# The weight split is emitted at the head of each step, ahead of the step's other work

## The chip, the cores and the metric

The kernel runs on one core of one Trainium2 chip. The metric is the time of one execution in microseconds (us): 2224.38 us, the median of three runs of the kernel before (2222.93 to 2225.11). A core has several engines, each with its own queue of instructions, which it works off in order: TensorE (PE in the profile) multiplies matrices, VectorE (DVE) and ScalarE (ACT) do elementwise work, GpSimd (POOL) does some elementwise work and issues some transfers, SyncE (SP) issues transfers. They wait for one another by semaphores.

## The reference

One decoder block on x of 256 tokens by 2048 channels, in float32, cut here to its chain:

```python
p = x @ w_in                          # 2048 x 9776, columns for all heads and gates
a = diff_attention(p)                 # 8 heads, value width 128 each
n = nsa_attention(p)                  # 16 heads, 4 KV groups: compressed, selected, window
m = sigmoid(g_da) * (a @ w_branch_da) + sigmoid(g_nsa) * (n @ w_branch_nsa)
h = layer_norm(alpha * x + m @ w_out)
# PEER: product keys choose 16 of 128 x 128 experts for each of 8 heads
s1, s2 = q1 @ sub_k1.T, q2 @ sub_k2.T         # q = h @ w_q
eid, gate = top16(top16(s1) + top16(s2))      # expert numbers, softmax of the scores
y = sum over heads, k: gate * gelu(u[eid] . h) * v[eid]
out = layer_norm(alpha * h + y)
```

u and v have 16384 rows (experts) of 2048 channels each. The tokens together choose so many rows that the kernel streams all of u and v and computes every expert for every token: act = gelu(u h), times a matrix G of 16384 experts by 256 tokens that holds the gates (zero where an expert was not chosen), and then G-weighted act times v.

## The kernel before

**One stream of weights.** All large matrices (w_in, the branch matrices, w_out, w_q, u, v) pass through one object W of class Stream as tiles of 128 partitions by 1024 float32 (512 KB). SyncE loads them into three raw buffers. TensorE multiplies in a rounded form of float32, so each tile is *split* into two: hi, a rounding cast by ACT (L98), and lo, the rest raw minus hi by DVE (L99). A tile has two halves of 512 columns, each with a cast and a subtraction; lo waits for hi. In a part of the program (`W.share`) GpSimd does the subtraction of the second half. The pools of hi and lo hold six halves, three tiles. A product is three passes, hi by hi, lo by hi, hi by lo; a tile takes 24 matmuls of 256 columns (in the v pass 12 of 512).

**One step a tile.** `step(fn)` handles one tile. `W.take()` hands out the tile whose turn it is (its split was emitted in an earlier step), `fn` emits its matmuls, and `W.ahead()` emits the split of the tile two places on (and the loads for which a raw buffer is free).

**Everything else rides on the steps.** Attention, top-k, the building of G and the weight split of the v pass are cut into slots (cost, pre, post), queued with `bg`. A step earns a credit (1 as a rule) and takes a slot when it has credit; the slot's pre (elementwise work) is emitted before the matmuls of the tile, its post (TensorE work) after them. Two more lists exist: `deferred` holds evacuations of PSUM, emitted by `flush()` at the start of the next step; `late` holds evacuations that are emitted in the next step after the slots (as `now`). There is no scheduler: instructions stand in each engine's queue in the order in which the code emits them.

**Stages in time**, from the profile: to 150 us the first columns of x @ w_in; to 350 the differential attention beside more of them; some 385 to 515 the NSA attention beside the gate columns; to 735 the merge, w_out and the first norm; to 970 w_q, and the first of u beside the top-k work; 970 to 1190 u beside the building of G; to 1500 the rest of u; to 2200 v; then the second norm.

**The attention pipeline.** `pipeline` (slots) has for unit k in one slot: pre does the softmax (`u_softmax`, L510 to L527) of unit k-1, the evacuation of the transposed weights (`u_evac`, L548 to L554) of unit k-3, the output (`u_out`, L584) of unit k-5; post does the logits of unit k, transposes (tp, L539) of k-2, pv of k-4.

**The G stage.** `g_onehot(q)` (pre; L1202, L1204) makes on DVE, from keys and gates in slotT, one-hot matrices `one` and `ob` for four tokens; `g_mm(q-1)` (post) multiplies those of the slot before into a bank `lg`, with eight small matmuls; its `ev` goes to `deferred` and is emitted first in the next step:

```python
V.scalar_tensor_tensor(g0[:, 0:n0, ts], gv[:, 0:n0, :], 1.0 / GSCALE, g0[:, 0:n0, ts], op0=OP.mult, op1=OP.mult)   # L1219
if n0 < HI:
    A.activation(g0[:, n0:HI, ts], gv[:, n0:HI, :], AF.Copy, scale=1.0 / GSCALE)   # L1222
A.activation(g1[:, :, ts], gv[:, HI:I2, :], AF.Copy, scale=1.0 / GSCALE)           # L1223
```

There are 64 such q; a slot costs GCOST = 1.05. In this stage a finished accumulator of u (every fourth step) is also evacuated in the flush, by a gelu on ACT (L1255) and a store that ACT issues (L1259).

Of the kernel before, what the change touches and what calls it, by code (L numbers as in the profile page):

```python
# [130 lines left out]
def block_kernel(ctx, tc, x, xT, w_in, rel_bias, onehot, lamq, lamk, subln_g, pe, w1, w2k, w2v, cmask,  # L131
# [11 lines left out]
    W = Stream(nc, stream, 3, 6)  # L143
# [6 lines left out]
    def flush(every=False):  # L150
        for q in (deferred, late) if every else (deferred,):
            for f in q:
                f()
            q.clear()

    def step(fn, credit=1.0):
        part = W.take()
        flush()
        now, late[:] = list(late), []
        state["c"] = min(state["c"] + credit, 2.0)  # L160
        post = None
        while credit and slots and state["c"] > 0 and post is None:
            cost, pre, post = slots.pop(0)
            state["c"] -= cost
            if pre:
                pre()
        for f in now:
            f()
        W.ahead()
        fn(*(part or ()))  # L170
        if post:
            post()
# [607 lines left out]
    for name, form, width, j, half in plan:  # L780
        if name == "x":
            step(lambda: None, half)
            continue
        if name == "w1":
            step(lambda hi, lo, kv=width, jj=j: w1_step(kv, jj, hi, lo), 0)
            continue
# [21 lines left out]
        if form == "T":  # L808
            def fn(hi, lo, j=j, half=half):
                if j == 0 and half == 0:  # L810
                    acc["b"] = [bank("acc", 4) for _ in range(2)]
                mm_T(acc["b"], hi, lo, xhi, xlo, 2 * j + half, 15)
            step(fn, 0.5 if name == "qd0" and j == 0 else 1)
            if j == 7:
                def ev(name=name, b=acc["b"]):
                    evac_T(name, b, 0)
                    late.append(lambda: evac_T(name, b, 1))
                late.append(ev)
        else:
            def fn(hi, lo, j=j, width=width):  # L820
                if j == 0:
                    acc["b"] = [bank("acc", 4) for _ in range(2)]
                mm_N([b[:, :width] for b in acc["b"]], hi, lo, xhi, xlo, 2 * j, (0, 1))
            step(fn, width / 512)
            if j == 7:
                late.append(lambda name=name, width=width, b=acc["b"]: evac_N(name, width, b))
# [677 lines left out]
```

## Time and profile before

| | |
|---|---|
| median of 3 runs | 2224.38 us (2222.93 to 2225.11) |
| profiled execution | 2224.97 us |
| its span | 2223.2 us |
| mean granted TensorE clock | 0.996 |
| busy: TensorE, weight loads | 2184.4 us (98%), 2016.0 us (91%) |
| busy: DVE, ACT, GpSimd | 1452.2 us (65%), 1130.3 us (51%), 246.5 us (11%) |
| chain that ended last | PE 75%, DVE 8%, DMA 5%, ACT 2% |
| 16 DMA engines | 424.72 MB, mean 191 GB/s |

The span runs from the first to the last instruction of the profiled execution; its own time is a little longer. Busy times are sums over instructions on an engine; matmuls overlap in the pipeline, so a busy TensorE is one with matmuls in flight. The granted clock is 1.00 where TensorE runs at 2.4 GHz, its higher level; the lower is 1.2 GHz. The chain is followed back from the last instruction, at each step to what released it.

### The profile page before, as it was taken

How to read it: one execution, taken by the hardware profiler on the slowest of the kernel's cores; microseconds unless marked ns; L12 is line 12 of the kernel's file. 1: busy time of each engine (PE TensorE's matmuls, PEld its weight loads, DVE VectorE, ACT ScalarE, POOL GpSimd, SP SyncE). 2: the span in 40 equal slices, each digit the busy share in tenths (PEclk: the TensorE clock that was granted, in tenths of full speed). 3: DMA queues.
4: the chain of work that ended last, by engine and by line, in shares of the span. 5: the costliest groups of instructions: out<-in, count | busy, mean ns of one | idle time of the engine just before them, and what ended most of it. 6: DMA issues, size and time to landing. Idle time of an engine off the chain costs nothing.

```text
span 2223.2 us, 40705 instructions
## 1 busy us (share of the span) xinstructions
PE 2184.4 (98%) x15712; PEld 2016.0 (91%) x15712; DVE 1452.2 (65%) x2898; ACT 1130.3 (51%) x2153; POOL 246.5 (11%) x223
## 2 busy tenths in 40 slices
PE   9999999999999999999999999999999999999997
PEld 9988999999987999999999999998888888888786
DVE  5558774665767889988886555555555555555567
ACT  5555654665545444455554444445555455554443
POOL 2002234443001501210000000000000000000002
PEclk9999999999999999999999999999999999999999
DMA  7664564545675766555656666666666666667774
GB/s 243 195 186 155 173 198 130 166 151 162 202 226 160 238 183 189 181 185 181 182 183 190 196 194 194 193 197 206 196 191 194 193 193 196 192 197 236 253 220 143
DMA packets 119843, 424.72 MB, mean 191 GB/s; under 512 B 13876, under 2 KB 14212, under 8 KB 119392
## 3 DMA queue, kind: packets, MB, share of 16 engines
q1 hardware_dynamic: 111600, 398.90, 58.0%
q0 software_dynamic: 5600, 18.75, 2.8%
q10 hardware_dynamic: 2448, 4.46, 0.5%
q8 instruction: 123, 2.02, 0.4%
q14 instruction: 72, 0.59, 0.1%
HBM read 413.37 MB, written 8.69 MB: 190 GB/s over the span
## 4 chain that ended last, share of the span: by engine, by line
PE 75%; DVE 8%; DMA 5%; ACT 2%; issue 2%; POOL 1%; ACTq 0%; DVEq 0%; POOLq 0%; SPq 0%
PE acc L191 43%; PE o L191 27%; DVE lo L99 4%; PE lg L191 2%; DMA raw<-in_v_dram 2%; DMA raw<-in_w_in_dram 1%; PE pv L191 1%; DMA raw<-in_wout_dram 1%; DMA raw<-in_wq_dram 1%; ACT hi L98 1%; PE tp L539 1%; DVE eq L1107 0%; DVE eid L1111 0%; DVE st L901 0%; DVE r L933 0%
## 5 line engine op out<-in xcount | busy, mean ns | idle before, releaser
L99 DVE TENSOR_TENSOR lo<-raw,hi 128x512 fp32r<-128x512 f32 (+1 forms) x1422 | 980.8, 719 | 551.2 <-ACT hi L98 549.2
L98 ACT CAST hi<-raw 128x512 fp32r<-128x512 f32 (+1 forms) x1494 | 872.4, 617 | 692.5 <-PE o L191 267.6
L191 PE MATMUL acc<-yhi,lo 128*128 128x256 f32 x2112 | 586.7, 278 | 5.5 <-DVE lo L99 5.5
L191 PE MATMUL acc<-yhi,hi 128*128 128x256 f32 x2112 | 591.4, 280 | 0.0
L191 PE MATMUL acc<-ylo,hi 128*128 128x256 f32 x2112 | 584.1, 277 | 0.0
L191 PEld LDWEIGHTS acc<-yhi,lo 128*128 128x128 f32 x2112 | 397.0, 188 | 9.4 <-DVE lo L99 9.1
L191 PEld LDWEIGHTS acc<-yhi,hi 128*128 128x128 f32 x2112 | 396.8, 188 | 0.4 <-ACT hi L98 0.2
L191 PEld LDWEIGHTS acc<-ylo,hi 128*128 128x128 f32 x2112 | 396.7, 188 | 0.0
L191 PE MATMUL o<-lo,whi 128*128 128x512 f32 x1000 | 389.7, 390 | 0.8 <-DVE lo L99 0.8
L191 PE MATMUL o<-hi,whi 128*128 128x512 f32 x1000 | 389.4, 389 | 0.6 <-ACT hi L98 0.5
L191 PE MATMUL o<-hi,wlo 128*128 128x512 f32 x1000 | 389.1, 389 | 0.0
L191 PE MATMUL acc<-xhi,hi 128*128 128x256 f32 x1024 | 290.7, 284 | 4.2 <-ACT hi L98 4.2
L191 PE MATMUL acc<-xhi,lo 128*128 128x256 f32 x1024 | 286.5, 280 | 5.5 <-DVE lo L99 5.3
L191 PE MATMUL acc<-xlo,hi 128*128 128x256 f32 x1024 | 285.2, 279 | 0.0
L191 PEld LDWEIGHTS o<-lo,whi 128*128 128x128 f32 x1000 | 187.7, 188 | 42.0 <-DVE lo L99 3.1
L191 PEld LDWEIGHTS o<-hi,whi 128*128 128x128 f32 x1000 | 187.7, 188 | 40.9 <-ACT hi L98 1.5
L191 PEld LDWEIGHTS o<-hi,wlo 128*128 128x128 f32 x1000 | 187.7, 188 | 38.5
L191 PEld LDWEIGHTS acc<-xhi,lo 128*128 128x128 f32 x1024 | 194.1, 190 | 7.8 <-DVE lo L99 7.7
L191 PEld LDWEIGHTS acc<-xhi,hi 128*128 128x128 f32 x1024 | 194.4, 190 | 6.0 <-ACT hi L98 5.6
L191 PEld LDWEIGHTS acc<-xlo,hi 128*128 128x128 f32 x1024 | 193.9, 189 | 0.0
L1282 POOL DMA_DIRECT2D back<-act_d x17 | 9.3, 546 | 1170.5 <-DVE G L1290 607.4
L99 POOL TENSOR_TENSOR lo<-raw,hi 128x512 fp32r<-128x512 f32 x72 | 104.1, 1450 | 231.7 <-ACT hi L98 228.0
(308 smaller groups left out, 2170.3 us busy)
## 6 DMA issues: line engine op xcount, KB each, us to landing
raw<-in_u_dram SPq DMA_DIRECT2D x256, 512.0 KB, 4.1
raw<-in_v_dram SPq DMA_DIRECT2D x256, 512.0 KB, 3.6
raw<-in_w_in_dram SPq DMA_DIRECT2D x143, 512.0 KB, 4.1
raw<-in_wout_dram SPq DMA_DIRECT2D x32, 512.0 KB, 4.2
raw<-in_wbda_dram SPq DMA_DIRECT2D x16, 512.0 KB, 3.9
raw<-in_wbnsa_dram SPq DMA_DIRECT2D x16, 512.0 KB, 3.8
raw<-in_wq_dram SPq DMA_DIRECT2D x16, 512.0 KB, 4.2
raw<-in_w_in_dram SPq DMA_DIRECT2D x16, 280.0 KB, 3.0
```

Source lines behind the costliest of these rows:

```text
L98: self.nc.scalar.copy(hi[:, :w], r)
L99: (self.nc.gpsimd if self.share and b else sub).tensor_tensor(lo[:, :w], r, hi[:, :w].bitcast(F32), op=OP.subtract)
L191: PE.matmul(o, a, b, start=start, stop=stop, skip_group_check=True)
L539: PE.transpose(tp[:, 128 * b:128 * b + 128], P[:, 128 * b:128 * b + 128], ident)
L1282: GP.dma_start(t, act_d[vorder[n]])
```

## The change

In `step`, `W.ahead()` moves from behind the slots' pre and the late evacuations to ahead of them; the flush stays first:

```diff
         part = W.take()
         flush()
         now, late[:] = list(late), []
+        W.ahead()
         state["c"] = min(state["c"] + credit, 2.0)
         post = None
         while credit and slots and state["c"] > 0 and post is None:
...
                 pre()
         for f in now:
             f()
-        W.ahead()
         fn(*(part or ()))
```

Each engine has as many instructions as before. The orders on TensorE and SyncE are the same; those of DVE, ACT and GpSimd differ. In the rows below a name's number is that of its buffer; numbers differ between the versions by a few, since buffers are numbered as they are emitted. `lo_...<-raw_...` is the subtraction of half a tile.

DVE's queue in the G stage, before: the evacuation L1219, the one-hot of the slot, then the split.

```order
L1219 SCALAR_TENSOR_TENSOR G0_9652<-lg_13661,G0_9652 128x34x4
L1202 TENSOR_TENSOR one_13673<-keys_12741,slotT_9401 128x1024
L1204 TENSOR_TENSOR ob_13674<-one_13673,slotT_9401 128x512 x2
L99 TENSOR_TENSOR lo_13679<-raw_13529,hi_13678 128x512
L99 TENSOR_TENSOR lo_13683<-raw_13529,hi_13682 128x512
L1219 SCALAR_TENSOR_TENSOR G0_9652<-lg_13712,G0_9652 128x34x4
L1202 TENSOR_TENSOR one_13724<-keys_12741,slotT_9401 128x1024
L1204 TENSOR_TENSOR ob_13725<-one_13724,slotT_9401 128x512 x2
```

The same place after, from the same evacuation on (lg_13661).

```order
L1219 SCALAR_TENSOR_TENSOR G0_9662<-lg_13661,G0_9662 128x34x4
L99 TENSOR_TENSOR lo_13674<-raw_13524,hi_13673 128x512
L99 TENSOR_TENSOR lo_13678<-raw_13524,hi_13677 128x512
L1202 TENSOR_TENSOR one_13683<-keys_12751,slotT_9401 128x1024
L1204 TENSOR_TENSOR ob_13684<-one_13683,slotT_9401 128x512 x2
L1219 SCALAR_TENSOR_TENSOR G0_9662<-lg_13712,G0_9662 128x34x4
L99 TENSOR_TENSOR lo_13725<-raw_13575,hi_13724 128x512
L99 TENSOR_TENSOR lo_13729<-raw_13575,hi_13728 128x512
```

The split of the same tile (raw_13529, now raw_13524) stands between the evacuation and the one-hot, no longer behind the one-hot. ACT's queue in this stage reads L1222, L1223, the two casts hi, in both versions, with L1255 and the store between L1223 and the casts in every fourth step.

DVE's queue in the NSA attention, before: a unit's softmax (its last rows), an evacuation, an output, the split of one half, the next softmax.

```order
L527 TENSOR_TENSOR rs_5207<-rs_5207,gsig_147 128x1
L549 SCALAR_TENSOR_TENSOR wt_5211<-tp_5180,wt_5211 128x384
L584 SCALAR_TENSOR_TENSOR r1_146<-pv_5184,rs_4909,r1_146 128x64 x2
L99 TENSOR_TENSOR lo_5217<-raw_5002,hi_5216 128x512
L510 ISA P_5280,nm_5278<-lg_5252,tb_5101 128x256
```

The same place after.

```order
L527 TENSOR_TENSOR rs_5217<-rs_5217,gsig_147 128x1
L549 SCALAR_TENSOR_TENSOR wt_5221<-tp_5180,wt_5221 128x384
L584 SCALAR_TENSOR_TENSOR r1_146<-pv_5184,rs_4919,r1_146 128x64 x2
L99 TENSOR_TENSOR lo_5279<-raw_5056,hi_5278 128x512
L510 ISA P_5290,nm_5288<-lg_5252,tb_5101 128x256
```

The row of lo is that of the next tile (raw_5056 in place of raw_5002); the other rows are the same, so that each of them stands behind one more split than before.

## Rows read from the trace of the kernel before

**Rows 1.** The page, part 1: busy time, share of the span, instructions

```profile
PE 2184.4 (98%) x15712; PEld 2016.0 (91%) x15712; DVE 1452.2 (65%) x2898; ACT 1130.3 (51%) x2153; POOL 246.5 (11%) x223
```

**Rows 2.** Waits of PE: waiter, releaser, us in total, times, longest

```profile
PE acc L191 <- DVE lo L99: 11.0, 19, 1.4
PE acc L191 <- ACT hi L98: 4.2, 3, 2.4
```

**Rows 3.** Windows: stretch: us, busy time of each engine, PEclk, DMA share, GB/s

```profile
970.00:1184.00 214.00, 214.00 (x2072) 211.79 (x2072) 184.15 (x385) 113.07 (x274) 1.23 (x1) 1.00 0.58 184
1250.00:1300.00 50.00, 50.00 (x444) 50.00 (x443) 26.61 (x42) 22.77 (x41) 0.00 (x0) 1.00 0.65 192
344.59:348.08 3.49, 3.49 (x35) 3.49 (x33) 0.38 (x1) 0.00 (x0) 0.00 (x0) 1.00 0.42 150
348.08:360.69 12.61, 12.61 (x99) 12.61 (x99) 8.93 (x18) 7.30 (x13) 5.42 (x4) 0.86 0.26 84
```

**Rows 4.** Waits from 970 to 1187 us, columns as in rows 2

```profile
ACT G L1222 <- DVE G L1219: 93.4, 63, 2.7
DVE lo L99 <- ACT hi L98: 15.0, 19, 1.1
DVE G L1219 <- PE lg L191: 12.1, 29, 0.7
```

**Rows 5.** Timelines of DVE and PE near 405 us: start, duration, instruction

```profile
405.57 0.47 DVE L584 SCALAR_TENSOR_TENSOR r<-pv,rs,r 128x64 f32<-128x64 f32 x2
408.18 0.60 PE L191 MATMUL pv<-vd,wt 128*128 128x64 bf16 x15
```

**Rows 6.** Timeline of PE from 203 to 208.5 us, its waits in brackets

```profile
205.42 0.52 PE L539 MATMUL tp<-ident,P 128*128 128x128 f32 x3 [1.76 <-DVE wt L554]
207.18 0.38 PE L191 MATMUL acc<-xhi,hi 128*128 128x256 f32 x1 [0.57 <-ACT hi L98]
207.99 0.39 PE L191 MATMUL acc<-xhi,lo 128*128 128x256 f32 x1 [0.43 <-DVE lo L99]
```

**Rows 7.** Timeline of PE near 268 us

```profile
268.08 0.40 PE L191 MATMUL acc<-hi,xhi 128*128 128x280 f32 x1 [0.81 <-ACT qs L390]
```

**Rows 8.** Timeline of DVE in the G stage

```profile
971.99 0.76 DVE L1204 TENSOR_TENSOR ob<-one,slotT 128x512 f16<-128x512 f16 x2
...
1000.99 1.29 DVE L99 TENSOR_TENSOR lo<-raw,hi 128x512 fp32r<-128x512 f32 x2 [0.73 <-ACT hi L98]
1002.20 0.29 DVE L1219 SCALAR_TENSOR_TENSOR G<-lg,G 128x136 f32<-128x136 f32 x1
...
1005.37 0.68 DVE L1202 TENSOR_TENSOR one<-keys,slotT 128x1024 f16<-128x1024 f16 x1
...
1006.76 1.29 DVE L99 TENSOR_TENSOR lo<-raw,hi 128x512 fp32r<-128x512 f32 x2
1008.44 0.30 DVE L1219 SCALAR_TENSOR_TENSOR G<-lg,G 128x136 f32<-128x136 f32 x1 [0.40 <-PE lg L191]
...
1011.74 0.30 DVE L1219 SCALAR_TENSOR_TENSOR G<-lg,G 128x136 f32<-128x136 f32 x1 [0.40 <-PE lg L191]
```

**Rows 9.** Timeline of ACT in the G stage

```profile
1000.33 1.14 ACT L98 CAST hi<-raw 128x512 fp32r<-128x512 f32 x2 [0.40 <-ACT act L1255]
...
1009.21 1.14 ACT L98 CAST hi<-raw 128x512 fp32r<-128x512 f32 x2
...
1013.50 1.14 ACT L98 CAST hi<-raw 128x512 fp32r<-128x512 f32 x2 [0.40 <-ACT act L1255]
```

**Rows 10.** Timeline of PE in the G stage, the lg matmuls

```profile
974.84 0.63 PE L191 MATMUL lg<-ob,one 128*128 128x128 f16 x8
...
1004.48 0.63 PE L191 MATMUL lg<-ob,one 128*128 128x128 f16 x8
...
1007.77 0.63 PE L191 MATMUL lg<-ob,one 128*128 128x128 f16 x8
```

**Rows 11.** Line L1219: count, duration ns min/median/max, first and last start

```profile
L1219 DVE SCALAR_TENSOR_TENSOR G<-lg,G x64: 290/300/301, 976.5 to 1188.4; 128x136 f32<-128x136 f32 x64
```

## The prediction

> **What bounds the kernel now.** I read the page first: TensorE is busy for 98% of the span, VectorE (DVE) for 65%, ScalarE (ACT) for 51% [rows 1]. Whatever DVE and ACT do is therefore free as long as TensorE never stands, and a change of order on them costs only where TensorE starts to wait. The waits of TensorE on a split are small: 11.0 us in 19 waits on lo, 4.2 us in 3 on hi [rows 2]. That is all that an earlier split can give back.
>
> Next I asked stage by stage how near the other engines are to TensorE. The table of windows answers it [rows 3]: from 1250 to 1300 us (the plain steps of the u pass) DVE is busy for 26.61 of 50 us, but from 970 to 1184 us, the stage that builds G from one-hot matrices, for 184.15 of 214 us, with TensorE at 214.00. That is 86%, the tightest long stage of the program, so I looked there for who waits for whom [rows 4]: ACT's L1222 waits for DVE's L1219 63 times, 93.4 us in all, DVE's lo waits for ACT's hi only 19 times, and DVE's L1219 waits for TensorE's lg 29 times. DVE and ACT hand work to each other in every step, and DVE still finds time to wait for TensorE.
>
> **The change part by part.** Instruction counts stay the same on every engine; the change moves casts (L98) and subtractions (L99) past other work, so it has no price but waits. It matters which work. In a step the evacuations put off from the step before (flush) come first in both versions; the work pieces (pre, and the late evacuations) stood between them and the split, and now stand behind it.
>
> *Pieces with slack.* Where a stage has no flush work on DVE or ACT, the rows on these engines are the same ring as before (piece, split, piece, split), each piece now one split later. A split wants its tile two steps before TensorE uses it, so what the splits gain is not needed where TensorE does not wait for them, and what the pieces lose is paid only where TensorE waits for a piece. In the NSA attention a step's output (L584, at 405.57 us, 0.47 us long) is done 2.14 us before the next pv matmul at 408.18 [rows 5]; one more subtraction of a half tile ahead of it takes some 0.6 us (half of the pair in [rows 8]; the other half is GpSimd's here). Cost 0, bounded by 0 and, if the lead is used up in each of the stage's some 37 steps and half a subtraction stands over, 37 x 0.3 = 11 us.
>
> *Pieces without slack.* In the differential attention at 205.42 us TensorE stands for 1.76 us on wt (DVE), and then for 0.57 and 0.43 us on hi and lo of the next tile [rows 6]. There the softmax comes later by a split and the split sooner: the first wait grows to about 3.5, the second and third go. Net +0.5, between -1 and +2. At 268.08 us TensorE stands for 0.81 us on qs (ACT) [rows 7]; a cast pair more ahead of it takes at most the 1.14 us of the 512-wide pair [rows 9], the tile here is 280 wide: +0.7, between 0 and 1.1. The 15.2 us of rows 2 I count as unchanged: these waits come in bursts where DVE or ACT is overloaded, and a reordering of one burst takes no work out of it. Bounds -15 and 0; I take 0, because the ring behind them is the same one.
>
> *The G stage.* Here a step's flush holds work for DVE and ACT: L1219 (DVE), then L1222, L1223 (ACT), which empty the lg bank into G. ACT's casts of the next split stand behind L1222 in both versions. L1222 starts when L1219 ends, whatever TensorE does: L1219 at 1002.20 and again at 1008.44 us [rows 8]; the cast follows the second at 1009.21 [rows 9]. DVE's order before is L1219, one-hot (L1202, L1204 twice), lo, lo: while ACT is at L1222, L1223 and hi, DVE has the one-hot to do, and lo finds hi ready. After, it is L1219, lo, lo, one-hot: DVE stands behind L1219 until ACT has emptied its part and cast hi, with the one-hot queued behind the standing lo. L1219 of the next step is behind the one-hot on the same engine. The step on DVE and ACT becomes one ring without overlap, summed from start to start:
> L1219 to hi: 1008.44 to 1009.21, 0.77 us [rows 8, 9].
> hi to lo: 1000.33 to 1000.99, 0.66 us (a step in which DVE was waiting for hi) [rows 8, 9].
> The pair of lo: 1000.99 to 1002.20, 1.21 us [rows 8].
> The one-hot: 1005.37 to 1006.76, 1.39 us [rows 8].
> Sum 4.03 us. TensorE needs from lg to lg 1004.48 to 1007.77, 3.29 us [rows 10]. So DVE with ACT becomes the bound, and TensorE will stand for some 0.7 us in each step, before lg on ob.
> In every fourth step ACT has the gelu of a finished accumulator and the issue of its store between L1223 and hi: L1219 to hi is 1011.74 to 1013.50, 1.76 us [rows 8, 9], the ring 5.02 us.
> L1219 runs 64 times from 976.5 to 1188.4 us [rows 11], 63 intervals, 211.9 us. After: 16 with gelu x 5.02 = 80.3, 47 without x 4.03 = 189.4. The slot costs 1.05 of a credit of 1 per step, so about two plain steps fall into the stage without a slot; TensorE's 24 matmuls take 2.70 us each time (3.29 less the 0.59 of lg), I take 2 more for each, +4. Sum 273.7, that is +61.8. The stage begins with the first one-hot at 971.99 + 0.76 = 972.75, 2.1 us ahead of its lg at 974.84 [rows 8, 10]; this lead is eaten first, -2.1. Net **+59.7 us**. Bounds: 0, if the ring does not close (below), and +90, if lo starts only at the end of hi's second cast (1.14 in place of 0.66, 63 x 0.48 = 30 more); I take 0.66, which is the row in which DVE stood and waited as it will.
>
> *Behind the G stage.* From 1190 us on the pieces are the weight splits of the v pass, which are used steps later, and DVE is half idle [rows 3]: 0.
>
> **Sum.** +59.7 + 0.5 + 0.7 = +60.9. The profiled execution took 2224.97 us (span 2223.2, 1.8 around it) and gives 2285.9; it lies 0.59 above the median of the three runs, 2224.38, so I forecast 2285.
>
> **The rivals.**
> *The ring does not close; no change.* If L1222 waited for TensorE's lg and not for L1219, ACT could cast hi while DVE is elsewhere; DVE's own work of a step, 0.30 + 1.21 + 1.39 = 2.9 us, lies below the 3.29 of TensorE, and the stage keeps its time. The point from which it decides is a ring under 3.29. For it: DVE's 29 waits for lg [rows 4] show spare time. Against: at 1002.20 L1219 ran late and lg had been finished for some time, and the 63 waits of L1222 name L1219. Time 2224 to 2227.
> *The other side: faster.* If lo of the early split stands in no burst (the queue of DVE has always work and hi is done ahead), the 11.0 + 4.2 us of rows 2 go and the G stage holds: 2224.4 - 15.2 = 2209. It decides where TensorE's wait for lo is caused by the piece ahead of it and not by hi. For it: lo is the first releaser of TensorE's waits. Against: it needs the open ring of the case above as well, and the waits are single ones (19) where both engines are full.
> *The clock falls in the G stage.* TensorE's standing of 0.7 us a step could bring its granted clock to the lower level, 1.2 GHz. From 348.08 to 360.69 us the trace shows a mean granted clock of 0.86, after 3.49 us of small matmuls (35 groups) at a clock of 1.00 [rows 3]. At the lower level a step's 3.29 us of matmuls take 6.58, then TensorE is the bound again and does not stand, so that the level would come back; for half of the 63 steps the sum is 63 x (0.5 x 6.58 + 0.5 x 4.28) = 342 us in place of 211.9, +130, about 2355. Against: waits of 1.76 us as in rows 6 are longer than those expected here. The Trainium skill (TensorE: Matmul & The Clock Gate, section "A second HAM failure mode: psum-queue depth-cycling") tells of a kernel whose TensorE stands briefly between groups of matmuls and whose clock swings between the two levels for it; by that rule this case would come about. Rows of this case show the clock at 1.00 over the whole G stage only without such standing [rows 3], so they neither show nor exclude it.
> *NSA loses its lead too.* The split of this stage has its second half on GpSimd, next to DVE, and pieces come later on both; with the bound of 11 us on top the time is 2296. The Trainium skill (SBUF — State Buffer, section "Who interferes with whom") says that DVE and GpSimd share a pair of ports under an exclusive lock, so that another alignment of their instructions could lengthen either. The row of GpSimd's lo would show it by a longer duration than before; no row of before separates it.
>
> **How the numbers follow.** A run can tell a change from none at about 0.2% (4.4 us). Forecast, the ring in the G stage and little else: 0.72, 2276 to 2293. NSA in addition: 0.10, to 2300. The clock: 0.06, 2310 to 2360. No change, or a ring that closes only in the gelu steps (16 x 1.7 = 28 us): 0.08, of which 0.05 within 0.2%. Faster: 0.04. The range takes in the first two cases and the upper part of the partial ring: 2258 to 2306. Slower 0.91, same 0.05, faster 0.04.
>
> **What would show it.** In the profile after: the L1219 rows spread from about 976 to some 1250 us, 4.0 us apart and 5.0 in every fourth; DVE's lo waits for ACT's hi in nearly each of the 64 steps (1.1 us each, 2.1 in gelu steps) and no longer for lg; TensorE has waits "lg on ob" of 0.5 to 0.9 us; the stretch from 1190 on has the same length as before; the waits on lo outside the stage stay near 11 us in total; the wait on wt near 205 us grows to 3 to 4 us and the two behind it go. I am wrong if L1219's interval stays at 3.3 us, if a granted clock below 1.00 stands in the stage, or if more than 10 us come from before 970 us.

## The result: 2285.46 us, 2.8% slower

The changed kernel takes 2285.46 us (median of 5 runs, 2284.13 to 2288.82) against 2223.54 us (5 runs, 2222.31 to 2225.11) before: ratio 1.0282, 95% interval 1.0271 to 1.0294, +61.9 us. Forecast were 2285 us and a range of 2258 to 2306.

The page after, part 1, answers to [rows 1]: the same instructions, TensorE's share down by two points.

```profile
PE 2200.6 (96%) x15712; PEld 2016.0 (88%) x15712; DVE 1450.6 (64%) x2898; ACT 1136.5 (50%) x2153; POOL 239.3 (10%) x223
```

The waits of PE in the profile after (us in total, times, longest) have two releasers that were not there before, ob and nm, and two that have grown, wt (1.8 us, one wait, before) and qs (0.8 us, one wait); lo and hi [rows 2] have fallen from 15.2 to 10.3 us together.

```profile
PE lg L191 <- DVE ob L1204: 33.8, 56, 1.3
PE acc L191 <- DVE lo L99: 8.8, 15, 1.4
PE lg L191 <- DVE nm L510: 4.3, 2, 2.5
PE tp L539 <- DVE wt L554: 3.7, 2, 2.1
PE acc L191 <- ACT qs L390: 2.2, 2, 1.9
PE acc L191 <- ACT hi L98: 1.5, 3, 0.9
```

The wait on ob is the G stage. Its window after (columns as in [rows 3]): TensorE was busy for all 214.00 us of the stage before, now for 240.66 of 280 us, at a granted clock of 1.00. Behind it a plain window of 50 us of u holds 443 matmuls, where it held 444 before: a step there costs what it cost.

```profile
970.00:1250.00 280.00, 240.66 (x2158) 222.22 (x2158) 190.68 (x400) 117.09 (x284) 1.51 (x1) 1.00 0.46 146
...
1300.00:1350.00 50.00, 50.00 (x443) 50.00 (x442) 26.74 (x42) 22.70 (x41) 0.00 (x0) 1.00 0.67 197
```

The waits of that stage (970 to 1252 us) beside [rows 4]: DVE's lo now waits for ACT's hi in nearly every step, 88.0 us in place of 15.0, and the wait of L1219 for lg is gone.

```profile
ACT G L1222 <- DVE G L1219: 155.4, 64, 2.6
DVE lo L99 <- ACT hi L98: 88.0, 65, 2.1
PEld L191 <- DVE ob L1204: 44.7, 56, 1.5
PE lg L191 <- DVE ob L1204: 33.8, 56, 1.3
```

Line L1219 after, beside [rows 11]: 270.1 us from first to last, where it was 211.9.

```profile
L1219 DVE SCALAR_TENSOR_TENSOR G<-lg,G x64: 290/291/293, 979.5 to 1249.6; 128x136 f32<-128x136 f32 x64
```

One step and the gelu step behind it, on DVE's timeline after (brackets: idle time before, and what ended it), beside [rows 8]:

```profile
1004.59 0.29 DVE L1219 SCALAR_TENSOR_TENSOR G<-lg,G 128x136 f32<-128x136 f32 x1
1006.00 1.29 DVE L99 TENSOR_TENSOR lo<-raw,hi 128x512 fp32r<-128x512 f32 x2 [1.12 <-ACT hi L98]
1007.21 0.68 DVE L1202 TENSOR_TENSOR one<-keys,slotT 128x1024 f16<-128x1024 f16 x1
...
1008.61 0.29 DVE L1219 SCALAR_TENSOR_TENSOR G<-lg,G 128x136 f32<-128x136 f32 x1
1011.02 1.29 DVE L99 TENSOR_TENSOR lo<-raw,hi 128x512 fp32r<-128x512 f32 x2 [2.12 <-ACT hi L98]
...
1013.63 0.29 DVE L1219 SCALAR_TENSOR_TENSOR G<-lg,G 128x136 f32<-128x136 f32 x1
```

From L1219 to L1219 it is 4.02 and 5.02 us (4.03 and 5.02 forecast): 1.41 us to lo, 1.21 for the pair, 1.40 for the one-hot.

The waits on nm, wt and qs are in the attention. PE's timeline after near the places of [rows 6, 7], and one new place at 392 us:

```profile
202.19 1.77 PE L191 MATMUL lg<-kdT,qdT 64*128 64x256 f32 x8 [2.47 <-DVE nm L510]
206.03 0.88 PE L539 MATMUL tp<-ident,P 128*128 128x128 f32 x3 [2.07 <-DVE wt L554]
...
250.07 0.52 PE L539 MATMUL tp<-ident,P 128*128 128x128 f32 x3 [1.67 <-DVE wt L554]
...
269.25 0.40 PE L191 MATMUL acc<-hi,xhi 128*128 128x280 f32 x1 [1.88 <-ACT qs L390]
...
392.14 0.47 PE L191 MATMUL lg<-khi,qs 128*128 128x512 f32 x1 [1.85 <-DVE nm L510]
```

The logits of a unit need the lg banks that the softmax of the unit before empties (L510). With a split ahead of it the softmax comes late, and TensorE waits for the bank before it can even reach the transposes. It stood for 2.47 us, did eight small matmuls and stood for 2.07 us. Its granted clock fell behind the first of the two: the mean from 202 to 205 us was 0.70, and from 205 to 208 us it was 0.50, the lower level. In the profile before, both windows have 1.00.

```profile
202.00:205.00 3.00, 1.77 (x8) 1.31 (x8) 1.77 (x10) 2.40 (x9) 0.51 (x1) 0.70 0.56 175
205.00:208.00 3.00, 1.97 (x10) 2.00 (x11) 2.32 (x5) 1.46 (x3) 1.61 (x4) 0.50 0.03 5
```

Where the time went, by the start of the same TensorE work in both profiles: the first lg matmul of the G stage came at 974.84 before and is 2.8 us later after, the last (1187.76) 59.0 us later; the v pass begins 59.2 us later, and the span is 59.1 us longer. So in this pair of profiles 56.2 us of the 59.1 lie in the G stage.

### The profile page after: what moved, and what is told of

It is laid out like the page before. It is cut to its first block, busy times and chain, and to the rows that moved or that the text cites. A ratio compares the mean times of both kernels' runs of the same rounds, so it can differ in the third digit from the quotient of the medians.

```text
span 2282.3 us, 40732 instructions
## 1 busy us (share of the span) xinstructions
PE 2200.6 (96%) x15712; PEld 2016.0 (88%) x15712; DVE 1450.6 (64%) x2898; ACT 1136.5 (50%) x2153; POOL 239.3 (10%) x223
## 4 chain that ended last, share of the span: by engine, by line
PE 62%; DVE 16%; ACT 6%; DMA 4%; issue 3%; POOL 0%; ACTq 0%; DVEq 0%; POOLq 0%; SPq 0%
PE acc L191 33%; PE o L191 27%; DVE lo L99 8%; ACT hi L98 2%; DVE one L1202 2%; DMA raw<-in_v_dram 2%; DVE ob L1204 1%; DMA raw<-in_w_in_dram 1%; PE pv L191 1%; PE lg L191 1%; ACT G L1223 1%; DMA raw<-in_wq_dram 1%; DMA raw<-in_wout_dram 1%; DVE G L1219 1%; ACT G L1222 1%
## 5 line engine op out<-in xcount | busy, mean ns | idle before, releaser
L99 POOL TENSOR_TENSOR lo<-raw,hi 128x512 fp32r<-128x512 f32 x72 | 97.7, 1360 | 238.1 <-ACT hi L98 237.2
```

Source lines behind the costliest of these rows:

```text
L99: (self.nc.gpsimd if self.share and b else sub).tensor_tensor(lo[:, :w], r, hi[:, :w].bitcast(F32), op=OP.subtract)
```

## The experiments

The theory: in the G stage DVE and ACT close a ring (L1219, ACT's part, hi, lo, one-hot, and L1219 of the next step) in which each piece waits for the one before. It takes 4.0 us a step, and TensorE, at 3.29, has to wait. The rival: the one-hot behind the split on DVE's queue is the loss by itself, whatever ACT does. For what is left outside the stage there are two candidates, the attention and the top-k work.

**Only the G stage.** In `step`, the other steps keep the old place:

```diff
+        g = bool(slots) and slots[0][0] == GCOST
+        if g:
+            W.ahead()
...
-        W.ahead()
+        if not (g):
+            W.ahead()
```

> The new order only in the steps of the G stage, the old order in all others. Theory (in the G stage DVE and ACT form a ring of 4.01 us a step against TensorE's 3.29): the whole loss comes back, +56 to +58 us on the kernel before, 2280 to 2282 us, with L1219 every 4.0 us and 5.0 us in gelu steps. Rival (the loss is spread over the program, a few us per stage, because pieces come later everywhere): less than +45.

Measured: 2277.8 us against 2222.89 of the kernel before in the same series, ratio 1.0249 (1.0234 to 1.0265), +54.9. The line of L1219 runs for 270.3 us, as in the changed kernel:

```profile
L1223 DVE SCALAR_TENSOR_TENSOR G<-lg,G x64: 290/292/294, 972.8 to 1243.1; 128x136 f32<-128x136 f32 x64
```

The stage alone is nine tenths of the loss; the time is 2 us below the expected band.

**All but the G stage**, the same edit with `not g`.

> The new order in all steps except those of the G stage. Theory: the G stage keeps its 212 us, and what is left is the sum of small shifts that the profile after shows (2.8 us late at the first lg matmul, then 0.9 won back in the v pass): +1 to +4 us, 2225 to 2227.5 us. Rival (the split that comes sooner takes waits away outside the G stage): at or below 2223 us. Rival (loss spread over the program): over 2235 us.

Measured: 2231.08 us, ratio 1.0038 (1.0025 to 1.0050), +8.2 against 2222.89. The G stage keeps its 212.2 us (983.4 to 1195.6). What is left outside is more than expected, though less than the rival of a spread loss, and about three times the 2.8 us that the pair of profiles shows (the interval is 5.6 to 11 us). That the earlier split wins something on balance outside the stage is refuted. Where these 8 us lie is taken up again below, with att_only.

**The casts ahead of the flush.** In the steps of the G stage only, on top of the change; DVE's order is untouched (`cast_ahead`, not shown, casts both halves of the next tile, and its split then uses these casts):

```diff
         part = W.take()
+        if slots and slots[0][0] == GCOST:
+            W.cast_ahead()
         flush()
```

> The changed kernel with one thing more: in the G stage ACT's two casts hi are emitted ahead of the flush, so that they stand before L1222 and no longer behind it; DVE's order is the changed one (L1219, lo, lo, one-hot). Theory (the ring closes through ACT: L1219, L1222, hi, lo): the ring is open, lo no longer stands behind L1219, a step takes TensorE's 3.3 us, 2226 to 2231 us. Rival (the one-hot behind the split on DVE's queue is the loss, whatever ACT does): L1219 still every 4.0 us, 2280 to 2290 us.

Measured: 2230.81 us, ratio 1.0036 (1.0023 to 1.0050). The loss of the stage is gone; what is left agrees with that of all_but_g. DVE's timeline shows the changed order at TensorE's pace, 3.3 us a step, and DVE has time to wait for lg again (L1234 is L1219 there):

```profile
1003.19 0.30 DVE L1234 SCALAR_TENSOR_TENSOR G<-lg,G 128x136 f32<-128x136 f32 x1 [0.40 <-PE lg L206]
1003.41 1.28 DVE L102 TENSOR_TENSOR lo<-raw,hi 128x512 fp32r<-128x512 f32 x2
1004.61 0.68 DVE L1217 TENSOR_TENSOR one<-keys,slotT 128x1024 f16<-128x1024 f16 x1
...
1006.49 0.30 DVE L1234 SCALAR_TENSOR_TENSOR G<-lg,G 128x136 f32<-128x136 f32 x1 [0.40 <-PE lg L206]
```

The one-hot behind the split costs nothing when hi is not behind L1219: the rival falls.

**ACT's L1222 on DVE**, on top of the change:

```diff
-                A.activation(g0[:, n0:HI, ts], gv[:, n0:HI, :], AF.Copy, scale=1.0 / GSCALE)
+                V.tensor_scalar(g0[:, n0:HI, ts], gv[:, n0:HI, :], 1.0 / GSCALE, None, op0=OP.mult)
```

> The changed kernel with ACT's L1222 (30 of 64 columns of G0) done by DVE, right behind L1219. No ACT instruction then writes the tile that L1219 writes, so ACT has nothing to wait for but TensorE's lg. Theory: L1223 and hi start at the end of lg and no longer after L1219, the ring is open, and although DVE has some 0.27 us more to do in each step (2.9 + 0.27 = 3.2 us, just under 3.29), the stage goes back to 3.3 to 3.4 us a step: 2227 to 2237 us. Rival (one-hot behind the split on DVE): DVE has more to do in the same order, 4.0 to 4.3 us a step, 2285 to 2303 us.

Measured: 2290.36 us, ratio 1.0304 (1.0289 to 1.0320): a miss, and inside the rival's band of 2285 to 2303, so that this run by itself does not tell the two theories apart; hi_first and act_first do. The ring did not open. ACT's L1223 writes another tile than DVE does, and still waits for DVE:

```profile
1004.83 0.29 DVE L1219 SCALAR_TENSOR_TENSOR G<-lg,G 128x136 f32<-128x136 f32 x1
1005.04 0.27 DVE L1222 TENSOR_SCALAR G<-lg 128x120 f32<-128x120 f32 x1
1006.33 1.29 DVE L99 TENSOR_TENSOR lo<-raw,hi 128x512 fp32r<-128x512 f32 x2 [1.02 <-ACT hi L98]
```

```profile
1005.41 0.38 ACT L1223 ACTIVATE G<-lg 128x256 f32<-128x256 f32 x1 [2.70 <-DVE G L1222]
1005.69 1.14 ACT L98 CAST hi<-raw 128x512 fp32r<-128x512 f32 x2
```

By the code, what the two engines share is the lg bank that both read; in the program as built the second reader waits for the first. So the tile G0, where the expectation put the wait, is not needed for it. The ring stands: summed anew from these rows it is 0.58 to L1223, 0.28 to hi, 0.64 to lo, 1.21, 1.40: 4.11 us, and the timeline has L1219 at 1004.83 and 1008.94, 4.11 us apart.

**ACT first.** On top of the change, the evacuation's parts in the order L1222, L1223, L1219:

```diff
-            V.scalar_tensor_tensor(g0[:, 0:n0, ts], gv[:, 0:n0, :], 1.0 / GSCALE, g0[:, 0:n0, ts],
-                                   op0=OP.mult, op1=OP.mult)
             if n0 < HI:
                 A.activation(g0[:, n0:HI, ts], gv[:, n0:HI, :], AF.Copy, scale=1.0 / GSCALE)
             A.activation(g1[:, :, ts], gv[:, HI:I2, :], AF.Copy, scale=1.0 / GSCALE)
+            V.scalar_tensor_tensor(g0[:, 0:n0, ts], gv[:, 0:n0, :], 1.0 / GSCALE, g0[:, 0:n0, ts],
+                                   op0=OP.mult, op1=OP.mult)
```

> The changed kernel with the parts of the G evacuation in another order: ACT's L1222 and L1223 first, then DVE's L1219. Orders of split and one-hot stay the changed ones. Theory (the ring needs ACT to stand behind DVE's L1219; the order of the two is what the shared lg bank fixes): ACT now empties the bank as soon as lg is done and casts hi while DVE is still busy, lo finds hi ready or nearly so, a step takes 3.3 us again: 2226 to 2233 us. Rival (the one-hot behind the split on DVE is the loss): 4.0 us a step, 2280 us and above.

Measured: 2230.38 us, ratio 1.0031 (1.0021 to 1.0041). Waits in the G stage (980 to 1200 us; in this kernel ACT's two parts are L1220 and L1221, and DVE's is L1222):

```profile
ACT G L1220 <- PE lg L191: 93.6, 64, 2.4
DVE lo L99 <- ACT hi L98: 25.8, 35, 1.3
DVE G L1222 <- ACT G L1221: 2.5, 3, 0.9
```

ACT now waits for TensorE's lg and not for DVE, and lo's wait is back from 88.0 to 25.8 us. Where DVE comes too early, it is now DVE that waits for ACT's read of the bank. A second way to open the same ring, with no instruction more or less, has the same result.

**L1223 issued twice**, in the changed kernel and in the kernel before:

```diff
             A.activation(g1[:, :, ts], gv[:, HI:I2, :], AF.Copy, scale=1.0 / GSCALE)
+            A.activation(g1[:, :, ts], gv[:, HI:I2, :], AF.Copy, scale=1.0 / GSCALE)
```

> The changed kernel with L1223 issued twice (the second writes the same values again), which puts 0.26 us more of ACT work between L1219 and hi in each of the 64 steps. Theory (ACT's work there lies on the ring): 4.01 + 0.26 = 4.27 us a step, 63 x 0.26 = +16 us, 2300 to 2303 us. Rival (DVE alone is the bound): no change, 2285 us.

> The kernel before with L1223 issued twice in the same way. Theory (in the old order this work lies beside DVE's one-hot): 0 to +3 us, 2223 to 2226 us. Rival (ACT's work counts in either order): +16 us, 2239 us.

Measured: 2313.79 us after (ratio 1.0411, 1.0395 to 1.0427) and 2223.08 us before (0.9999, 0.9990 to 1.0008; 2223.8 in the series). The same work is free in the one order and costs some 28 us in the other. The size expected after, 16 us, was too small because I took L1223's distance to hi for the price of another L1223; its distance to its own repetition is larger. ACT's timeline:

```profile
1003.90 0.38 ACT L1223 ACTIVATE G<-lg 128x256 f32<-128x256 f32 x1
1004.32 0.39 ACT L1224 ACTIVATE G<-lg 128x256 f32<-128x256 f32 x1
1004.60 1.13 ACT L98 CAST hi<-raw 128x512 fp32r<-128x512 f32 x2
```

0.42 us more on the ring; 63 x 0.42 = 26.5, and L1219 runs for 296.6 us (980.2 to 1276.8), 26.5 more than in the changed kernel. In this kernel the granted clock of the stage is no longer full:

```profile
980.00:1277.00 297.00, 243.29 (x2081) 226.49 (x2080) 182.06 (x381) 135.11 (x335) 0.00 (x0) 0.95 0.41 130
```

**Attention only, and the rest only.** The edit of g_only with another condition for the early split (two kernels, one line for each):

```diff
-        if g:
+        if W.pos <= 160:                # att_only
+        if W.pos > 160 and not g:       # late_only
             W.ahead()
```

> The new order only in the first 160 steps (the columns of x @ w_in with both attentions, to some 515 us), the old order after them. Theory (outside the G stage the loss stands mostly here: the logits wait for a bank that the softmax behind a split empties late, near 202 and 392 us, and TensorE's clock falls after the first of them): +3 to +7 us on the kernel before, 2226 to 2230 us. Rival (it stands in the top-k stage from 735 to 970 us): within 1.5 us of the kernel before.

> The new order only after the first 160 steps, and not in the G stage (merge, w_out, w_q, top-k, the rest of u, v). Theory (what all_but_g lost beyond att_only stands in the top-k stage, where DVE is the fullest): +2 to +5 us on the kernel before, 2226 to 2229 us, with the shift between 735 and 970 us in the profile. Rival (the loss outside the G stage is the attention's alone): within 1.5 us of the kernel before.

Measured: att_only 2227.79 us, ratio 1.0020 (1.0011 to 1.0029), +4.0; late_only 2223.89 us, ratio 1.0006 (0.9996 to 1.0016), not told from none, so its expectation failed. The waits of PE in att_only hold the same pair as in the changed kernel,

```profile
PE lg L194 <- DVE nm L513: 4.3, 2, 2.5
```

with the line numbers shifted by three; every kernel here with the new order in the attention has this row, and in the kernel before, g_only, late_only and twice_before TensorE has no wait on nm.

TensorE does the same work in the same order in all twelve kernels, so a stretch between two pieces of its work can be compared over all their profiles, one execution each. The first mark is the first matmul lg<-gd,relb, the second the last of lg<-klo,qs at the end of the attention, the third the first lg of the G stage. Before (the third mark is at 974.84):

```profile
L310 PE MATMUL lg<-gd,relb x2: 482/490/498, 39.3 to 39.6; 64*24 64x383 f32 x2
L191 PE MATMUL lg<-klo,qs x32: 274/340/398, 384.4 to 503.0; 128*128 128x512 f32 x16, 128*128 128x256 f32 x16
```

And after:

```profile
L310 PE MATMUL lg<-gd,relb x2: 482/490/499, 37.2 to 37.6; 64*24 64x383 f32 x2
L191 PE MATMUL lg<-klo,qs x32: 280/338/398, 383.0 to 503.5; 128*128 128x512 f32 x16, 128*128 128x256 f32 x16
L191 PE MATMUL lg<-ob,one x512: 217/218/233, 977.7 to 1247.4; 128*128 128x128 f16 x171
```

From the first mark to the second, the four kernels with the old order in the attention (before, twice_before, g_only, late_only) take 461.6 to 465.0 us and the eight with the new order 465.7 to 472.9 us: 5.3 us more in the mean. From the second to the third, the four with the old order there (before, twice_before, g_only, att_only) take 470.7 to 471.8 us and the eight with the new one 471.4 to 474.7 us: 2.1 us more. Together that is 7.4 us, which agrees with the 8.2 of all_but_g. The pair of profiles hid part of it: the profile of the kernel before reached the first mark at 39.3 us, later than each of the other eleven (37.2 to 38.5 us), whatever their order, so the 2.8 us counted from the start are 5.0 counted from that mark. In the second stretch TensorE has one wait in all eight and in none of the four, 0.7 us for sel before a transpose; the rest of the 2.1 us there is not explained.

**The split ahead of the flush too**, in all steps.

```diff
         part = W.take()
+        W.ahead()
         flush()
...
-        W.ahead()
         fn(*(part or ()))
```

> A third order for the whole program: the split ahead of the flush too. Theory: in the G stage the casts stand ahead of L1222 on ACT and the pair lo ahead of L1219 on DVE, so no ring closes, 3.3 us a step; the work pieces stand as late as in the changed kernel, so its loss outside the G stage stays: 2227 to 2234 us. Rival (a split that is never behind other work takes away waits of TensorE): under 2222 us, faster than both.

Measured: 2227.84 us, ratio 1.0016 (1.0007 to 1.0025). The G stage takes 210.7 us (985.4 to 1196.1), so no ring closes; the two waits on nm are there, 4.3 us, and with them a loss of the attention. No kernel here is faster than the one before beyond its interval.

## Why the prediction was right, point by point

**Bound and place.** TensorE bound, the G stage the tight one: right. 56.2 of the 59.1 us by which the span grew in the profiles lie there, and alone it makes +54.9 us.

**The ring's terms** were right to 0.02 us: 4.03 and 5.02 us forecast, 4.02 and 5.02 read. Between the first and the last L1219 I had +61.8 us, the profile has +58.2. Most of the difference is in what I added for the two steps without a slot: the two intervals that hold them took 5.22 us, 1.20 more than the others and not 2, and the last interval, behind which there is no one-hot any more, took only 2.62. The lead of 2.1 us was eaten as forecast: the last lg is 59.0 us late, the last L1219 61.2.

**Why L1222 waits for L1219**: the prediction took the wait from the rows and gave no reason. The expectation of dve_evac had it as a hand-over between the two writers of G, and failed; that run shows that the bank lg, which both engines read, is enough for it. The forecast did not depend on the reason.

**Pieces with slack, 0; pieces without, +1.2**: the step that failed, though it left the total inside the range. The ring of rows is the same, but I looked only for what a late softmax does to the output (L584) and to wt, and not at the third thing that hangs on it, the lg bank that it empties for the next logits. TensorE stood for it 4.3 us in two places, for wt 2.07 and 1.67 us (a second place, at 250 us, was not forecast; 3.5 us were, at the first, and there the two waits behind it went as forecast), for qs 1.88 in place of 0.81 + 0.7. Some of it is paid back by fewer waits on lo and hi (15.2 to 10.3 us in all), which I had at no change. By the runs, att_only has +4.0 us (2.4 to 6.4) and all_but_g 8.2 us (5.6 to 11), against +1.2 forecast for all of it. Between the two some 4 us are left that late_only (-0.9 to 3.6) by itself neither shows nor excludes. The marks in the twelve profiles put 5.3 us into the attention and 2.1 us between it and the G stage, where the prediction had nothing; what makes most of these 2.1 us stays open.

**The two errors cancel in part**: 59.7 us for the G stage are 3.5 too many, and 1.2 us for all the rest are some 6 to 7 too few. That the total of 2285 meets the median within 0.5 us is luck; that the G stage comes out at 56.2 us for 59.7 is not.

**The rivals.** No change and faster: refuted in g_only and all_but_g. (By its own sum of 28 us, a ring that closes only in the gelu steps would have given 2252, below the range that was to take in its upper part.) The clock: it did fall, but elsewhere and with little effect. In the changed kernel's G stage, where TensorE stands for 0.6 us a time before lg (33.8 us in 56 waits), the level stayed at 1.00; with L1223 twice, where a step takes 4.44 us and TensorE stands for 0.97 us a time (48.6 us in 50 waits), the mean fell to 0.95, and the time still followed the ring of DVE and ACT, so the lower clock only filled time in which TensorE had to stand anyway. The rule of the Trainium skill (TensorE: Matmul & The Clock Gate, section "A second HAM failure mode: psum-queue depth-cycling") agrees with the stage with L1223 twice and not with the changed kernel's. In the attention it fell to 0.50 after TensorE had stood for 2.47 us. The rows from 344.59 us that the prediction used hold 35 matmuls, not 35 groups. NSA's lead held: a wait on its outputs appears nowhere among TensorE's waits; its one new wait is the bank at 392 us. GpSimd's half of lo did not become longer there either: from 385 to 515 us it takes 1284 ns in the mean, 1489 before.

## What to carry to other kernels

When a step's order is changed, draw for each tight stage the ring of hand-overs between the elementwise engines and sum it from start to start; this stage had 14% of idle time on DVE and still became 27% longer, since the order decides whether hand-overs lie beside work or in the ring. Where two engines share an evacuation, ask which of them others wait for next: here, with ACT first, the earlier split no longer slowed the stage (2230.38 us in place of 2285.46); ACT first with the old place of the split was not run. For every piece that comes later, list all that it releases: not only its output but also the PSUM bank that it empties.

## What was not expected of the hardware and the program

Two engines that only read the same PSUM bank were serialised in this program: in dve_evac ACT's L1223, whose output is another tile, waited 2.70 us for DVE's last read of lg. No run here leaves that wait out, so whether the chip needs it is not shown. Two ACT instructions of 0.38 us that write the same place start 0.42 us apart, where L1223 and an independent instruction behind it start 0.26 to 0.28 us apart; why is not shown. And in the stage with L1223 twice, where TensorE is not the bound, a granted clock of 0.95 cost nothing that the ring had not already cost.
